# Hybrid decoder trunk on one core: other priorities for the parts of both mixers, and small DVE operations priced as users of the port shared with POOL

## The chip, the cores and the metric

The kernel runs on one core of one Trainium2 chip. The metric is the device time of one execution in microseconds (us); lower is better. A core has five engines that run at the same time, each through its own queue in order: TensorE (PE: matrix products and transposes), VectorE (DVE), ScalarE (ACT), GpSimd (POOL) and SyncE (SP, which here issues all DMA transfers). An engine waits for another through semaphores. Products land in banks of PSUM, and DVE or ACT move them to SBUF ("evict" them) before a bank can be used again. POOL and DVE share a port to SBUF.

## The reference

Two layers over a sequence of 512 rows of 1024 numbers, in float32. Each layer has a mixer, an MLP and a gated embedding, with layer norms between.

```python
for i in range(DEPTH):                       # DEPTH = 2
    m = _even_mixer(...) if i % 2 == 0 else _odd_mixer(...)
    x = _layer_norm(DN_ALPHA * x + m, ln1_g[i], ln1_b[i])
    x = _layer_norm(DN_ALPHA * x + _sq_relu_mlp(x, w_up[i], w_down[i]), ln2_g[i], ln2_b[i])
    gate = jax.nn.sigmoid(x @ ple_w_gate[i] + ple_b_gate[i])
    x = x + gate * (p[i] @ ple_w_proj[i])
```

The even mixer projects x once and feeds two kinds of attention. Eight latent heads (MLA) take queries from a query latent of 384 columns and keys and values from a kv latent of 256 columns; both latents are divided by their root mean square first. A rotary part of 32 columns is added to queries and keys. Eight sliding-window heads (SWA, window 128) share two key and value heads, with a table of relative position biases on the logits and a learned sink to each softmax. The odd mixer has sixteen causal heads whose logits get a cumulated forget gate. Each mixer ends in an output projection.

## The kernel before

**Numbers.** Every float32 value that enters a product is split into a rounded part ("hi", by a cast on ACT) and the rest ("lo", a subtraction on DVE or POOL); a product is three matmuls (hi·hi, hi·lo, lo·hi) into one bank (`mm3`). Weights come as pieces of up to 128 x 1024 through `piece`: a DMA into `raw`, a cast to `wh` (line 551), a subtraction to `wl` (line 488, on POOL or DVE as `SPLIT` and `on_pool` say). The function `weights` runs five pieces ahead; the operations that load and split a piece are recorded in the part that asked for weights at that moment. There are two `raw` buffers and twelve `w` buffers (six pieces).

**Stages.** The start loads x and three pieces and makes the shared keys and two of four sliding-window query pairs. Then come the even mixer's parts, its output projection with the first layer norm, the MLP with the second, the gated embedding, and the same with the odd mixer for the second layer.

**Parts.** `EVEN` and `ODD` list the parts of the two mixers. In the even one: `q` (projection of one pair of window queries; `q_stack`, lines 751 to 755, evicts it in two halves with two ACT casts and one DVE subtraction each), `kv` and `qn` (the latents' inputs, one block of 128 rows each; line 1016 copies the block), `ckv` and `cq` (division by the root mean square and transposes: line 1022, `rsqrt` with lines 631 to 640, POOL's scaling on line 1026, the products' eviction on lines 1036 and 1037), `rk` (rotation and transposes of the rotary key; lines 1058 and 1060 evict them as `kh` and `kl`), `bias` (the table of biases and the sinks), `c` (three DMA loads: the rotary tables and the causal mask), `v` (values), `r` (rotary queries, line 926), `mk` and `mq` (keys and queries of a pair of latent heads; `mq` also copies rotary rows by eight DMAs), `s` and `m` (one sliding-window or latent head: logits, softmax, transposes, product with the values), `os` and `om` (splits of the heads' outputs). In the odd one: `Q`, `K`, `V` (projections), `G` (forget gates), `F` (one head), `O` (split of outputs).

**What sets the order.** The program first records all operations with their engine, an estimated duration, and what they read and write (`Plan.op`). An operation's priority is its place in the record plus the shift of its part, and the smallest goes first:

```python
o.seq = len(self.ops)
o.prio = o.seq + self.shift
```

`Plan.schedule` then plays the program through on estimated durations. At each step it takes the engine that can go on first and, of that engine's operations that are ready at that time (inputs made, buffers free), the one with the smallest priority. Operations marked `port` share one more resource, and the delay is added after the choice:

```python
if o.port:
    t = max(t, port_free)
    port_free = t + o.dur
```

The order found in this way is fixed on each engine by dependences; on the chip an engine runs its operations in that order, whatever the actual durations are. In the kernel before, all operations on POOL are marked `port`, and on DVE those large ones that take all their inputs from SBUF (`tt`, and `split` with `psum=False`, and lines 1226, 1237, 1417, 1418). The weight pieces lie in memory in the order of the lists' names, not by priority.

**Layer norm** (`layer_norm`, lines 1220 to 1237): per block of 128 rows, sums of squares on ACT (line 1223), then a few operations on a single column: `nm` (1220), `va` (1228), a square root on ACT (1231), a reciprocal (1232), and one Newton step (1233 to 1235). Two large operations per half finish it (1226 and 1237), and PE transposes the result (line 523).

Of the kernel before, what the change touches and what calls it, by code (L numbers as in the profile page):

```python
# [34 lines left out]
ALU = mybir.AluOpType  # L35
# [12 lines left out]
        (5, 10, ((0, 1, 2), (3, 4, 5), (6, 7))),  # L48
        (10, 16, ((0, 1), (2, 3), (4, 5), (6, 7))))

EVEN = ("q1 bias+484 kv0-292 kv1-60 qn0+452 kv2-296 kv3+64 rk-132 qn1-692 qn2+272 qn3-104 s0+164 s1+292 ckv-156 "
        "c-204 q3-240 s2-124 s3-36 v0-56 s4+204 s5+224 cq-392 v1-84 s6+8 v2-84 v3-96 os0-204 r-72 s7+56 mk0+784 "
        "mq0-520 m0-284 m1+104 mk1+132 mq1-104 os3+804 os2-220 m2+132 m3-28 mk2-108 mq2-448 om0-192 m4-156 "
        "os1+1028 m5-260 mk3-276 om2+36 mq3-188 m6-104 m7-212 om3+144 om1-580").split()
ODD = ("Q0+88 V0-104 V1-240 V2+400 V3+1404 V4+1280 V5+2072 V6+1060 V7-1396 G+4 V8-196 V9-156 V10+704 K0-812 "
       "K3-1684 F0-304 Q4+1704 Q1-880 K1-420 F2+236 V11-1204 F1-1376 Q2-468 K2+360 F4-456 F5+120 K4+1484 F3-644 "
       "Q3+68 F6-1352 F7-384 F8-1156 K7+280 F9-372 Q5+332 K5-184 F10-1236 Q6-1004 F11-172 K6+68 F12-268 Q7+68 "
       "F13+44 O4-2576 O3+1208 F14-564 O0-532 F15-68 O5-704 O6-492 O2+840 O1-404 O7+2500").split()
EVEN_Q = 2
START = "x0 002 x1 104 x2 024 204 048 x3 x5 x4 x6 148 x7 248".split()  # L60
WARM = 8
# [4 lines left out]
def parts(order):  # L66

    for x in order:
        name, i, shift = re.fullmatch(r"([A-Za-z]+)(\d*)([+-]\d+)?", x).groups()
        yield name, [int(i)] if i else [], int(shift or 0)  # L70
# [23 lines left out]
def weight_pieces():  # L94
# [58 lines left out]
    own = {"q": e_q, "kv": e_kv, "qn": e_qn, "v": e_v, "r": e_r, "mk": e_mk}  # L153
    for name, i, _ in parts(EVEN):
        if name in own:
# [16 lines left out]
    def o_q(j, b=0):  # L172
        add(D, lambda I: _cols(I["od_w_in"][0], slice(b + j * P, b + (j + 1) * P)))

    own = {"V": o_v, "Q": o_q, "K": lambda j: o_q(j, D)}
    for name, i, _ in parts(ODD):
        if name in own:
# [250 lines left out]
def t_pe(n):  # L428
    return max((n + 32) / 2.4, 109.5) * 1e-3


class Trunk:
# [194 lines left out]
    def rsqrt(self, y, v, r, w, n=1, scale=0):  # L627

        t, hv = self.small("nt", n), self.small("nh", n)
        d = lambda fn, rr, ww, dur=0.07: self.dve(1, fn, rr, ww, dur=dur)  # L630
        d(lambda e: e.tensor_scalar(y().bitcast(I32), v().bitcast(I32), 1, None, ALU.arith_shift_right), r, [w])
        d(lambda e: e.tensor_scalar(hv[:], v(), -0.5 / 4 ** scale, None, ALU.mult), r, [hv])
        d(lambda e: e.tensor_scalar(y().bitcast(I32), y().bitcast(I32), -1, 0x5F3759DF + (scale << 23), ALU.mult, ALU.add), [], [w])
        for _ in range(3):
            if n == 1:
                d(lambda e: e.tensor_scalar(t[:], y(), y(), hv[:], ALU.mult, ALU.mult), [w, hv], [t], 0.19)
            else:
                d(lambda e: e.tensor_tensor(t[:], y(), y(), ALU.mult), [w], [t])
                d(lambda e: e.tensor_tensor(t[:], t[:], hv[:], ALU.mult), [hv], [t])
            d(lambda e: e.scalar_tensor_tensor(y(), t[:], 1.5, y(), ALU.add, ALU.mult), [t], [w])  # L640
# [137 lines left out]
    def even(self):  # L778
        self.start()
        for name, i, self.p.shift in parts(EVEN):  # L780
            getattr(self, "e_" + name)(*i)
# [55 lines left out]
    def e_bias(self):  # L837

        A, nc = self.A, self.nc
        oh = self.load("u", (P, 384), lambda: A["onehot"], "oh")  # L840
        rb = self.load("u", (P, P), lambda: A["relb"], "rb")
        pe = self.bank("o")
        self.pe(4 * t_pe(384), lambda: [nc.tensor.matmul(pe[:, :384], rb[:], oh[:], start=True, stop=True)], [rb, oh], [pe])
        et = self.u("e", F, (P, 384))
        self.dve(384, lambda e: e.tensor_copy(et[:], pe[:, :384]), [pe], [et])
        for i in range(2):
            self.dma(196608, lambda i=i: (self.scratch["e"].rearrange("(h i r w) -> i h r w", h=8, i=2, r=16)[i], et[:]),
                     [et], [(self.dram["e"], i)])
        self.sinks = self.load("sm16", (P, 8), lambda: A["sinks"].broadcast_to([P, 8]), "sinks")
        self.nsinks = self.p.buf("sm16", (P, 8), F, "nsinks")  # L850
        self.dve(8, lambda e: e.tensor_scalar(self.nsinks[:], self.sinks[:], -1.0, None, ALU.mult), [self.sinks], [self.nsinks])

    def e_q(self, j):
        b = self.bank("mm")
# [274 lines left out]
    def odd(self):  # L1129
# [5 lines left out]
        self.fq, self.fk, self.fo = {}, {}, {}  # L1135
        for name, i, self.p.shift in parts(ODD):
            getattr(self, "o_" + name.lower())(*i)
# [77 lines left out]
    def layer_norm(self, x, st, g, b):  # L1215

        nm, q, v, y = (self.small(n, 4) for n in ("nm", "sq", "va", "rs"))
        c = lambda z: z[:, 0:1]
        d = lambda fn, r, w, dur=0.07: self.dve(1, fn, r, w, dur=dur)
        d(lambda e: e.tensor_scalar(c(nm), st[:, 0:1], st[:, 1:2], -1.0 / D, ALU.add, ALU.mult), [st], [nm], 0.1)  # L1220
        for h in range(2):
            junk = self.u("junk")
            self.act(S, lambda e, h=h, junk=junk: e.activation(junk[:], x[h][:], AF.Square, bias=c(nm), accum_out=q[:, h:h + 1]),
                     [x[h], nm], [junk, (q, h)], aps=2)
        for h in range(2):
            self.dve(S + 57, lambda e, h=h: e.scalar_tensor_tensor(x[h][:], x[h][:], c(nm), g[h][:], ALU.add, ALU.mult),
                     [nm, g[h]], [x[h]], port=True)
        d(lambda e: e.scalar_tensor_tensor(c(v), q[:, 0:1], D * EPS, q[:, 1:2], ALU.add, ALU.add), [q], [v], 0.1)

        hv, t = self.small("hv", 4), self.small("nt", 4)  # L1230
        self.act(1, lambda e: e.activation(c(t), c(v), AF.Sqrt, scale=1.0 / D), [v], [t])
        d(lambda e: e.reciprocal(c(y), c(t)), [t], [y], 0.1)
        d(lambda e: e.tensor_scalar(c(hv), c(v), -0.5 / D, None, ALU.mult), [v], [hv])
        d(lambda e: e.tensor_scalar(c(t), c(y), c(y), c(hv), ALU.mult, ALU.mult), [y, hv], [t], 0.19)
        d(lambda e: e.scalar_tensor_tensor(c(y), c(t), 1.5, c(y), ALU.add, ALU.mult), [t], [y], 0.1)
        for h in range(2):
            self.dve(S + 57, lambda e, h=h: e.scalar_tensor_tensor(x[h][:], x[h][:], c(y), b[h][:], ALU.mult, ALU.add),
                     [y, b[h]], [x[h]], port=True)
# [255 lines left out]
```

## Time and profile before

| what | value |
|---|---|
| median of 3 runs | 1263.97 us (1263.49 to 1265.16) |
| the profiled execution's own time | 1265.41 us |
| its span, first to last instruction | 1263.6 us |
| PE busy | 1233.4 us (98%) |
| DVE busy | 949.7 us (75%) |
| ACT busy | 687.2 us (54%) |
| POOL busy | 505.2 us (40%) |
| mean granted clock of TensorE | 0.995 |

A busy share is an average over stages with different limits. A row of instructions gives its start and length in us, the engine, the line of the kernel, the operation, its tiles (out<-in), its shapes and, in brackets, how long the engine stood idle before it and what ended that. A row of waits gives the engine and line that waited, what it waited for, the total in us, the number of times and the longest. The line is often that of a helper: line 512 is every matmul of `mms`, 523 every transpose, 488 every `tt`, 502 and 503 the two halves of `split`.

### The profile page before, as it was taken

The page shows a single profiled execution, that of the slowest core. Times are in us where ns is not written, and L with a number is a line of the kernel's source. Part 1 is how long each engine was busy: PE and PEld are TensorE (multiplying, and loading weights), DVE is VectorE, ACT ScalarE, POOL GpSimd, SP SyncE. Part 2 cuts the span into 40 slices and gives each one's busy share as a digit, 9 for nine tenths or more (in the row PEclk, how much of TensorE's full clock was granted, in tenths as well). Part 3 has the DMA queues.
Part 4 walks back from the last instruction along what each step waited for, and adds up shares of the span by engine and source line. Part 5 has one row for each costly group of instructions (what it writes and reads, how often), then busy time and mean ns, then how long its engine had stood idle before and what let it go on. Part 6 is the DMA issues. An engine that isn't in the chain of part 4 may idle for free.

```text
span 1263.6 us, 17349 instructions
## 1 busy us (share of the span) xinstructions
PE 1233.4 (98%) x6108; PEld 1042.6 (83%) x6108; DVE 949.7 (75%) x1695; ACT 687.2 (54%) x1352; POOL 505.2 (40%) x408
## 2 busy tenths in 40 slices
PE   8988999999999999999999999899999999999998
PEld 6987888988888887888897888788888888888887
DVE  5568877899888887585543587868899878897564
ACT  5658874645444445353444697945654554445451
POOL 2545432444445444312213466331544545443120
PEclk9999999999999999999999999999999999999999
DMA  5422432233223422423232422352223332332131
GB/s 197 141 88 85 145 122 85 83 101 123 89 89 100 133 75 76 154 65 131 91 104 93 147 70 92 134 183 68 84 84 114 120 100 84 117 117 82 68 117 50
DMA packets 46791, 132.83 MB, mean 105 GB/s; under 512 B 5984, under 2 KB 8672, under 8 KB 46704
## 3 DMA queue, kind: packets, MB, share of 16 engines
q1 hardware_dynamic: 46704, 131.72, 31.6%
q8 instruction: 48, 0.79, 0.3%
q14 instruction: 39, 0.32, 0.1%
HBM read 126.03 MB, written 4.62 MB: 103 GB/s over the span
## 4 chain that ended last, share of the span: by engine, by line
PE 81%; ACT 8%; DVE 6%; issue 2%; DMA 2%; POOL 1%; SPq 0%; ACTq 0%; DVEq 0%; POOLq 0%
PE mm L512 31%; PE s L512 21%; PE t L512 16%; PE o L512 10%; ACT t L664 2%; PE t L523 2%; ACT wh L551 1%; DVE wl L488 1%; DMA raw<-in_wall_dram 1%; ACT pth L502 1%; DVE qlo L753 1%; ACT q L755 1%; ACT q L752 1%; DVE t L659 1%; POOL wl L488 0%
## 5 line engine op out<-in xcount | busy, mean ns | idle before, releaser
L488 POOL TENSOR_TENSOR wl<-raw,wh 128x1024 fp32r<-128x1024 f32 (+4 forms) x78 | 182.4, 2340 | 405.5 <-ACT wh L551 376.4
L551 ACT CAST wh<-raw 128x1024 fp32r<-128x1024 f32 (+5 forms) x150 | 152.2, 1018 | 148.0 <-DMA raw<-in_wall_dram 73.7
L488 POOL TENSOR_TENSOR wf<-raw,wf 128x512 fp32r<-128x512 f32 x84 | 122.1, 1475 | 173.4 <-ACT wf L584 156.8
L512 PE MATMUL mm<-xh,wh 128*128 128x512 f32 (+1 forms) x416 | 161.7, 389 | 2.8 <-DVE k L766 0.8
L512 PE MATMUL mm<-xl,wh 128*128 128x512 f32 (+1 forms) x416 | 159.6, 384 | 0.2 <-DVE xl L503 0.2
L512 PE MATMUL mm<-xh,wl 128*128 128x512 f32 (+1 forms) x416 | 159.7, 384 | 0.0
L488 DVE TENSOR_TENSOR wl<-raw,wh 128x1024 fp32r<-128x1024 f32 (+4 forms) x72 | 102.5, 1423 | 47.8 <-ACT wh L551 38.3
L584 ACT CAST wf<-raw 128x512 fp32r<-128x512 f32 x168 | 100.9, 615 | 34.9 <-PE t L512 15.3
L512 PE MATMUL t<-wf,rh 128*128 128x512 f32 x336 | 103.8, 390 | 0.7 <-DVE x L1350 0.7
L673 POOL TENSOR_SCALAR t<-t,st 128x256 f32<-128x256 f32 (+3 forms) x128 | 69.3, 561 | 79.3 <-DVE st L670 61.4
L512 PEld LDWEIGHTS mm<-xh,wh 128*128 128x128 f32 x416 | 78.8, 189 | 19.7 <-ACT q L755 2.2
L512 PEld LDWEIGHTS mm<-xh,wl 128*128 128x128 f32 x416 | 78.7, 189 | 15.8 <-DVE wl L503 0.4
L512 PEld LDWEIGHTS mm<-xl,wh 128*128 128x128 f32 x416 | 78.7, 189 | 14.4 <-DVE xl L503 0.5
L488 DVE TENSOR_TENSOR wf<-raw,wf 128x512 fp32r<-128x512 f32 x84 | 77.4, 936 | 17.4 <-ACT wf L584 17.1
L512 PE MATMUL mm<-wh,xh 128*128 128x384 f32 (+5 forms) x232 | 82.8, 357 | 5.9 <-DVE qlo L753 2.8
L512 PE MATMUL mm<-wl,xh 128*128 128x384 f32 (+5 forms) x232 | 80.6, 348 | 0.2 <-POOL wl L488 0.2
L512 PE MATMUL mm<-wh,xl 128*128 128x384 f32 (+5 forms) x232 | 80.7, 348 | 0.0
L1350 DVE TENSOR_TENSOR x<-x,t 128x512 f32<-128x512 f32 x100 | 67.0, 679 | 12.3 <-PE t L512 10.3
L664 ACT ACTIVATE t<-t,st 128x256 f32<-128x256 f32 (+3 forms) x128 | 68.7, 540 | 12.7 <-DVE st L659 10.6
L512 PEld LDWEIGHTS t<-wf,rh 128*128 128x128 f32 x336 | 62.8, 188 | 14.7 <-DVE x L1350 1.8
L512 PE MATMUL s<-wf,rh 128*128 128x512 f32 x224 | 69.0, 389 | 0.0
L512 PE MATMUL t<-wf,rl 128*128 128x512 f32 x168 | 65.4, 389 | 0.0
(296 smaller groups left out, 3273.9 us busy)
## 6 DMA issues: line engine op xcount, KB each, us to landing
raw<-in_wall_dram SPq DMA_DIRECT2D x183, 512.0 KB, 3.5
ck<-scratch_c SPq DMA_DIRECT2D x16, 256.0 KB, 3.8
raw<-in_wall_dram SPq DMA_DIRECT2D x9, 384.0 KB, 3.3
x<-in_xT_dram SPq DMA_DIRECT2D x8, 256.0 KB, 5.3
x<-in_xn_dram SPq DMA_DIRECT2D x8, 256.0 KB, 5.3
g<-in_rows_dram SPq DMA_DIRECT2D x8, 256.0 KB, 5.1
b<-in_rows_dram SPq DMA_DIRECT2D x8, 256.0 KB, 5.3
scratch_x<-x SPq DMA_DIRECT2D x8, 256.0 KB, 2.0
```

What stands on the lines that cost most here:

```text
L488: fn = lambda e: e.tensor_tensor(out(), a(), b(), op)
L502: self.act(n, lambda e: e.copy(hi(), src()), r, w, psum)
L512: return [self.nc.tensor.matmul(o(), a(), b(), start=s, stop=e, **kw) for o, a, b, s, e in prods]
L523: lambda: [self.nc.tensor.transpose(o(), i(), self.ident[:]) for o, i in items],
L551: self.act(w, lambda e: e.copy(hi[:, :w], raw[:, :w]), [raw], [hi])
L584: self.act(512, lambda e: e.copy(t[:, h[0]], src()), [key], [(t, 0)])
L659: return e.tensor_tensor_reduce(t[:, offs[i] + a:offs[i] + z], b[:, c + a:c + z], ad(), -scale, init, ALU.add, ALU.min, nm[:, i:i + 1])
L664: self.act(n, lambda e, i=i, tt=tt: e.activation(tt(), tt(), AF.Exp, bias=nm[:, i:i + 1], scale=-1.0, accum_out=sm[:, i:i + 1]), [(nm, i)] ...
L673: self.pool(0.13 + 1.21e-3 * n, lambda e, i=i, tt=tt: e.tensor_scalar(tt(), tt(), rc[:, i:i + 1], 1.0, ALU.mult, ALU.mult), [rc], [(t, i)])
L752: self.act(S, lambda e, q2=q2, rs=rs: e.copy(q2[rs, :], bank[rs, :]), [bank], [(q2, 0)], True)
L753: self.dve(S, lambda e, q2=q2, lo=lo, rs=rs: e.tensor_tensor(lo[rs, :], bank[rs, :], q2[rs, :].bitcast(F), ALU.subtract), [bank, (q2, 0)], ...
L1350: self.dve(S, lambda e, b=b, xx=xx: e.tensor_tensor(xx[:], xx[:], b[:], ALU.add), [b], [xx])
```

## The change

All parts stay in the same order of names, so the record and the weights' layout are the same; the shifts of 51 of 52 even parts and 24 of 53 odd parts change. In three places the small operations of DVE are recorded with `port=True`: in `rsqrt`, for `nsinks` in `e_bias`, and in `layer_norm`.

```diff
-EVEN = ("q1 bias+484 kv0-292 kv1-60 qn0+452 kv2-296 kv3+64 rk-132 qn1-692 qn2+272 qn3-104 s0+164 s1+292 ckv-156 "
-        "c-204 q3-240 s2-124 s3-36 v0-56 s4+204 s5+224 cq-392 v1-84 s6+8 v2-84 v3-96 os0-204 r-72 s7+56 mk0+784 "
-        "mq0-520 m0-284 m1+104 mk1+132 mq1-104 os3+804 os2-220 m2+132 m3-28 mk2-108 mq2-448 om0-192 m4-156 "
-        "os1+1028 m5-260 mk3-276 om2+36 mq3-188 m6-104 m7-212 om3+144 om1-580").split()
-ODD = ("Q0+88 V0-104 V1-240 V2+400 V3+1404 V4+1280 V5+2072 V6+1060 V7-1396 G+4 V8-196 V9-156 V10+704 K0-812 "
-       "K3-1684 F0-304 Q4+1704 Q1-880 K1-420 F2+236 V11-1204 F1-1376 Q2-468 K2+360 F4-456 F5+120 K4+1484 F3-644 "
-       "Q3+68 F6-1352 F7-384 F8-1156 K7+280 F9-372 Q5+332 K5-184 F10-1236 Q6-1004 F11-172 K6+68 F12-268 Q7+68 "
-       "F13+44 O4-2576 O3+1208 F14-564 O0-532 F15-68 O5-704 O6-492 O2+840 O1-404 O7+2500").split()
+EVEN = ("q1+12 bias+556 kv0-1128 kv1+20 qn0+440 kv2-244 kv3-156 rk-164 qn1-672 qn2-440 qn3-576 s0-116 s1+300 "
+        "ckv+132 c+536 q3-836 s2+108 s3+84 v0+16 s4+204 s5+956 cq-404 v1-160 s6+80 v2-32 v3-164 os0+532 r-68 "
+        "s7+152 mk0+2040 mq0-1268 m0+4 m1+236 mk1+184 mq1+16 os3+1272 os2-292 m2+224 m3-116 mk2+136 mq2-668 "
+        "om0-432 m4-608 os1+1368 m5-92 mk3-188 om2-4 mq3-1240 m6-72 m7-100 om3+216 om1-376").split()
+ODD = ("Q0+88 V0-104 V1-168 V2+400 V3+1404 V4+1280 V5+2072 V6+1020 V7-1396 G-76 V8-196 V9-156 V10+524 K0-812 "
+       "K3-1604 F0-304 Q4+1764 Q1-888 K1-420 F2+236 V11-1204 F1-1216 Q2-468 K2+352 F4-456 F5+120 K4+1404 F3-652 "
+       "Q3+68 F6-1352 F7-384 F8-1136 K7+248 F9-212 Q5+332 K5-144 F10-1236 Q6-1004 F11-552 K6+68 F12-276 Q7+68 "
+       "F13+44 O4-2436 O3+1428 F14-744 O0-840 F15+72 O5-656 O6-492 O2+840 O1-396 O7+2500").split()
@@ rsqrt
-        d = lambda fn, rr, ww, dur=0.07: self.dve(1, fn, rr, ww, dur=dur)
+        d = lambda fn, rr, ww, dur=0.07: self.dve(1, fn, rr, ww, dur=dur, port=True)
@@ e_bias
-        self.dve(8, lambda e: e.tensor_scalar(self.nsinks[:], self.sinks[:], -1.0, None, ALU.mult), [self.sinks], [self.nsinks])
+        self.dve(8, lambda e: e.tensor_scalar(self.nsinks[:], self.sinks[:], -1.0, None, ALU.mult), [self.sinks], [self.nsinks], port=True)
@@ layer_norm
-        d = lambda fn, r, w, dur=0.07: self.dve(1, fn, r, w, dur=dur)
+        d = lambda fn, r, w, dur=0.07: self.dve(1, fn, r, w, dur=dur, port=True)
```

## The prediction, made before the changed kernel ran

> **What bounds the kernel now.** I read the page first, then the busy time by stage, then what TensorE (PE) waited for in each stage. The first two rows are the page's, the others the busy time of each engine in five stretches (granted clock and DMA share at the end).
>
> ```profile
> span 1263.6 us, 17349 instructions
> PE 1233.4 (98%) x6108; PEld 1042.6 (83%) x6108; DVE 949.7 (75%) x1695; ACT 687.2 (54%) x1352; POOL 505.2 (40%) x408
> ```
> ```profile
> 0.00:30.00 30.00, 26.34 (x93) 18.16 (x94) 16.12 (x24) 16.53 (x26) 6.80 (x15) 0.94 0.60 197
> 30.00:190.00 160.00, 149.82 (x857) 132.93 (x857) 118.03 (x314) 117.23 (x293) 73.51 (x96) 0.98 0.36 117
> 190.00:630.00 440.00, 438.02 (x2083) 367.27 (x2082) 347.04 (x492) 213.37 (x374) 171.51 (x102) 1.00 0.31 100
> 630.00:840.00 210.00, 201.11 (x1095) 173.09 (x1094) 137.13 (x391) 140.83 (x309) 94.59 (x106) 1.00 0.36 118
> 840.00:1263.60 423.60, 418.12 (x1987) 351.13 (x1985) 331.38 (x476) 199.26 (x353) 158.83 (x91) 1.00 0.28 93
> ```
>
> PE sets the end: it is idle for 1263.6 - 1233.4 = 30.2 us in all. An order of work can only move idle time and slow stretches of PE, so the places are the even mixer behind its start (30 to 190 us, 10.2 us idle) and the odd mixer (630 to 840 us, 8.9 us). The start's 3.7 us belong to loads that neither list orders. Who ended PE's waits, in us, times and longest, first in 30 to 190, then in 630 to 840:
>
> ```profile
> PE mm L512 <- DVE ql L503: 4.3, 4, 3.2
> PE mm L512 <- DVE kl L1060: 2.1, 1, 2.1
> PE mm L523 <- DVE qlo L753: 1.2, 1, 1.2
> PE mm L512 <- DVE qlo L753: 0.9, 1, 0.9
> ```
> ```profile
> PE t L523 <- DVE ptl L503: 3.0, 3, 1.1
> PE mm L512 <- DVE qlo L753: 1.6, 2, 0.8
> PE s L512 <- DVE st L659: 1.2, 1, 1.2
> PE s L512 <- ACT q L755: 1.0, 1, 1.0
> ```
>
> Two waits are long, and both are for a "mm" bank that VectorE (DVE) had not emptied: 2.06 us before 66.19 and 3.17 us before 118.37. Behind each comes a second cost. These are PE's rows at the two places, and the windows after them (the third number from the end is the granted clock):
>
> ```profile
> 66.19 0.41 PE L512 MATMUL mm<-wh,xh 128*128 128x384 f32 x1 [2.06 <-DVE kl L1060]
> 118.37 0.76 PE L512 MATMUL mm<-ch,wh 128*128 128x512 f32 x1 [3.17 <-DVE ql L503]
> ```
> ```profile
> 67.00:70.40 3.40, 3.40 (x12) 3.40 (x11) 3.40 (x9) 2.26 (x11) 3.40 (x6) 0.50 0.00 0
> 118.20:121.60 3.40, 3.23 (x9) 2.68 (x10) 3.25 (x10) 2.53 (x10) 2.04 (x5) 0.50 0.47 112
> ```
>
> For 3.4 us after each of these waits the clock is 0.50, which costs 3.4 x 0.5 = 1.7 us more. The shorter waits have no such stretch: the clock of 0.98 over the 160 us is 3.2 us lost, these two and no third. So the first place costs 2.06 + 1.7 = 3.8 us and the second 3.17 + 1.7 = 4.9 us, together 8.7 of the 13.6 us (10.2 idle, 3.4 of slow clock) that any order of the even mixer could win. The Trainium skill (TensorE: Matmul & The Clock Gate, section "Why this matters for your kernels") asks for no idle gaps over about 3 us between bursts of matmuls; here 2.06 us was enough, so the trace differs and its row is used. By the page alone the first place would be worth 2.06 us, and the time 1261.9.
>
> **The change part by part.** No instruction comes or goes; only the order on each engine does, as the planner now prices and ranks it.
>
> *The port.* 121 operations now count as users of the port shared with GpSimd (POOL): 12 in each of the two `rsqrt` calls, `nsinks`, and 6 in each of 16 layer norms. Do they block? Rows of the lines concerned, with durations in ns as least/median/greatest:
>
> ```profile
> L638 DVE TENSOR_TENSOR nt<-rn x6: 156/162/2400, 59.3 to 89.9; 128x4 f32<-128x4 f32 x6
> ```
> ```profile
> L1228 DVE SCALAR_TENSOR_TENSOR va<-sq x16: 145/151/2384, 203.9 to 1209.1; 128x1 f32<-128x1 f32 x16
> ```
> ```profile
> L851 DVE TENSOR_SCALAR nsinks<-sinks x1: 1955/1955/1955, 18.7 to 18.7; 128x8 f32<-128x8 f32 x1
> ```
>
> They do: an operation of 0.16 us lasts up to 2.40 us. The longest `nt` sits just ahead of the first long wait. DVE's order there, and POOL's operation of that time:
>
> ```profile
> 61.17 2.40 DVE L638 TENSOR_TENSOR nt<-rn 128x4 f32<-128x4 f32 x1
> ...
> 64.08 0.68 DVE L503 TENSOR_TENSOR ptl<-t,pth 128x512 fp32r<-128x512 f32 x1
> 64.68 1.37 DVE L1060 TENSOR_TENSOR kl<-mm,kh 32x512 fp32r<-32x512 f32 x2
> ```
> ```profile
> 61.15 2.40 POOL L488 TENSOR_TENSOR wl<-raw,wh 128x1024 fp32r<-128x1024 f32 x1 [4.14 <-ACT wh L551]
> ```
> ```profile
> 61.64 1.16 ACT L1058 CAST kh<-mm 32x512 fp32r<-32x512 f32 x2
> 62.82 0.58 ACT L716 COPY ol<-o 64x512 f32<-64x512 f32 x1
> 63.42 0.48 ACT L502 CAST pth<-t 128x384 fp32r<-128x384 f32 x1
> ```
>
> POOL's split of q3's weight piece holds `nt` from 61.17 to 63.57, inside the reciprocal root of the kv latent. `kl`, which frees the bank, has had its input since 62.8 but stands behind `ptl`, and `ptl` waits for `pth` until 63.90. Bounds: with the block gone and the order kept, `ptl` could start at about 63.95 instead of 64.08, a gain of 0.13 us; with `kl` ahead of `ptl` and no block, `kl` could run from 62.8 to 64.2, PE would start 1.9 us sooner, the wait would be 0.2 us, and the slow stretch would not come: 3.8 us. The lower side is also open: more such blocks could fall elsewhere (a rival). I take 3.8 us, because what stood around the place is moved apart. A part's rank is the number of operations before it plus its shift. By count, `ckv` (this root) goes from 168 to 456, behind `s0` and `cq`; `kv0`, which carries q3's weight split, from -156 to -992; `qn2` from 510 to -202 and `qn3` from 144 to -328; `rk`, which holds `kl`, stays early (90 to 58).
>
> *Layer norms.* Four of 16 `va` are blocked (2.36 to 2.38 us). PE feels two of them:
>
> ```profile
> 230.00 0.55 PE L523 MATMUL t<-ident,x 128*128 128x128 f32 x3 [0.92 <-DVE x L1237]
> ```
> ```profile
> 878.69 0.55 PE L523 MATMUL t<-ident,x 128*128 128x128 f32 x3 [0.88 <-DVE x L1237]
> ```
>
> Bounds: -1.8 us if both go, +1.8 us if each doubles. I take 0: the planner picks by rank and readiness first and only then adds the port's delay, so `va` still follows `x` in line, and those ranks do not change.
>
> *q3.* It goes from 116 to -480, ahead of `cq` (112). Its 24 matmuls of 0.227 us cost the same anywhere; its bank does not. Its first and last evictions, and PE's wait for the bank:
>
> ```profile
> 90.42 0.58 ACT L752 CAST q<-mm 64x512 fp32r<-64x512 f32 x1 [1.42 <-PE mm L512]
> ...
> 93.55 0.69 DVE L753 TENSOR_TENSOR qlo<-mm,q 64x512 fp32r<-64x512 f32 x1 [1.24 <-ACT q L755]
> 94.39 0.52 PE L523 MATMUL mm<-ident,cn 128*128 128x128 f32 x3 [1.20 <-DVE qlo L753]
> ```
>
> The bank is held from 90.42 to 94.24, 3.82 us, of which other work (value products, `ckv`'s products, sink heads) hides all but 1.20. Bounds: -1.20 if the new neighbours hide it all, 3.82 - 1.20 = +2.6 if nothing does, and +1.7 for the slow clock on top. I take 0: a move with cover on both sides.
>
> *mq0, mq3, m4, c, s5.* `mq0` (151 to -597) and `mq3` (757 to -295) cannot run before the query latent and, for their rotary rows, part `r`; each issues 8 copies of about 0.6 us on the DMA queue (SP). `c` (149 to 889) issues three loads there, with about 60 us to spare now, so a later issue costs nothing until it is later than its 3.9 us of landing before `r`; then `r` and all eight heads wait. The first copy, and the rows of these loads and their first user:
>
> ```profile
> 111.72 0.62 SPq L495 DMA_DIRECT2D qh<-rh  x1
> ```
> ```profile
> L926 DVE TENSOR_TENSOR rt<-mm,rope x4: 680/686/692, 106.9 to 109.6; 128x512 f32<-128x512 f32 x4
> L495 SPq DMA_DIRECT2D rope<-in_rope_dram x2: 422/425/428, 43.2 to 43.6; - x2
> ...
> DMA to landing us min/median/max: 3.9/3.9/4.0
> ```
>
> Weight loads queue behind these copies on SP, but the pieces are fetched five ahead. `m4` passes `m0` (712 to 260, against 402 to 690) and `s5` sinks (709 to 1441). These re-deal the second long wait (4.9 us) without a row that says how. Bounds -4.9 and +4.9 (a second of its kind); I take 0.
>
> *Odd mixer.* 29 of 53 shifts stay and 15 move by 80 or less (a head has 37 operations); the largest moves are `F11` (-380), `O0` (-308) and `O3` (+220). The longest waits there are 1.2 us, none slows the clock. Bounds: half of the 8.9 us idle either way would be 4.4; I take 0 and let about 1.2 us (one wait) into the spread.
>
> **Sum.** -3.8 (first place) + 0 + 0 + 0 + 0. The profiled execution took 1265.41 us, of which 1263.6 is span and 1.8 lies around it; it becomes 1261.6. The median of the runs shown is 1263.97, 1.44 below it; the forecast is 1263.97 - 3.8 = 1260.2.
>
> **Rivals.**
> *Deeper (D):* the second long wait goes too. For it: it is a `ql` behind work of other parts on ScalarE (ACT), and `mq0` and `mq3` now outrank these. Against: `r`, which they need, stays where it was. 1260.2 - 4.9 = 1255.3.
> *Re-dealt (N):* waits of the same total elsewhere; the change does not do what it says, since planned order decides and the block meets another small operation. For it: the two `rsqrt` calls make 24 small operations, and POOL is busy 73.5 of 160 us there. 1264.0.
> *Slower (S):* q3 is evicted with nothing to hide it. One mechanism: both "mm" banks are full while `qn` or `kv` blocks want one, the 3.82 us hold is bare, and the clock halves behind it. It decides once PE's other work in the hold is under 1.8 us (a wait over 2 us). Price with the first place kept: 3.82 - 1.20 + 1.7 = +4.3, so 1268.3. For it: at -480 q3 stands among `qn` and `kv`, all users of the two banks, and sink heads, which hid it, are few that early. Against: its weight piece is loaded behind `qn`'s.
> *Over-priced (R):* some of the 121 never block. At 563.75 a reciprocal of the layer norm ran through in POOL's operation:
>
> ```profile
> 563.75 0.15 DVE L1232 RECIPROCAL rs<-nt 128x1 f32<-128x1 f32 x1
> ```
> ```profile
> 562.10 2.42 POOL L488 TENSOR_TENSOR wl<-raw,wh 128x1024 fp32r<-128x1024 f32 x1 [5.42 <-ACT wh L551]
> ```
>
> The planner now delays such operations by up to 2.4 us that the chip does not, so work that could go first stands behind them; doubling PE's two waits on `x` gives +1.8, so 1265.8. The Trainium skill (SBUF — State Buffer, section "Who interferes with whom") says that a DVE instruction with at most one SBUF input, outside its two-port modes, does not contend with GpSimd; by that rule this is R's case, and the reciprocal agrees at 0.15 us.
>
> **Chances.** Forecast 0.36, D 0.19, N 0.17, R 0.05, S 0.23. A measurement of this kernel tells about 0.2%, 2.5 us. Faster is the forecast and D, 0.55; within 0.2% is N and R, 0.22; slower is S, 0.23. The forecast's own range is 1258.5 to 1261.4. The range of 8 in 10 goes from D with 1.5 us below it (the odd mixer's one wait and a little) to S with 0.5 above: 1253.8 to 1268.8. It leaves out the far ends: both long waits and all layer-norm waits gone, or `c` landing late.
>
> **What would show it.** Right: no wait for `kl` over 1 us and no window at clock 0.50 between 60 and 75 us; PE idle in the even mixer down by about 2 us; PE busy time down by the slow stretch (1.7). Layer norms: `va` still at 2.38 four times, waits on `x` near 0.9. S: a `qlo` wait over 2 us before 100 us with a slow window behind it. D: one slow window fewer still. R: longer waits on `x`. The forecast is wrong if the slow windows after 30 us remain two, whatever became of `nt`.

## The result, and the profile after

The changed kernel takes 1256.81 us (median of 6 runs, 1256.37 to 1260.08) against 1263.84 us for the kernel before (median of 6 runs, 1262.53 to 1265.16). The ratio is 0.9947, with a 95% interval of 0.9935 to 0.996: faster by 5.1 to 8.2 us, most likely 6.7. The forecast was 1260.2 us in a range of 1253.8 to 1268.8. One execution of one later kernel (1525.14 us at a mean clock of 0.752, where the others of that kernel have 0.995 to 0.999) is left out of its time below.

The first two rows below are those of the page of the changed kernel, the others the busy time of each engine in the same five stretches as before, with TensorE's granted clock as the third number from the end.

```profile
span 1255.1 us, 17347 instructions
...
PE 1231.3 (98%) x6108; PEld 1040.5 (83%) x6108; DVE 943.9 (75%) x1695; ACT 686.9 (55%) x1352; POOL 505.5 (40%) x408
```
```profile
0.00:30.00 30.00, 27.54 (x105) 19.35 (x106) 17.37 (x25) 18.34 (x29) 6.79 (x15) 1.00 0.62 209
30.00:190.00 160.00, 152.07 (x872) 134.31 (x871) 123.25 (x320) 116.57 (x292) 73.81 (x96) 0.99 0.38 120
190.00:630.00 440.00, 438.11 (x2096) 368.34 (x2095) 341.22 (x490) 214.50 (x378) 171.56 (x101) 1.00 0.30 99
630.00:840.00 210.00, 203.93 (x1095) 174.78 (x1095) 135.63 (x395) 139.49 (x304) 96.73 (x106) 1.00 0.36 120
840.00:1255.10 415.10, 409.63 (x1948) 343.75 (x1946) 326.41 (x467) 197.97 (x351) 156.57 (x90) 1.00 0.29 93
```

PE is idle for 1255.1 - 1231.3 = 23.8 us, 6.4 less than before. In the even mixer (30 to 190 us) the idle time is 7.9 in place of 10.2 us, in the odd mixer (630 to 840 us) 6.1 in place of 8.9; the two long stages between and behind them barely differ. What PE waited for in the two mixers of the changed kernel (total, times, longest, in us):

```profile
PE mm L512 <- DVE ql L503: 3.9, 3, 2.7
PE mm L523 <- DVE qlo L753: 1.2, 1, 1.2
PE mm L523 <- DVE vsw L503: 1.1, 1, 1.1
...
PE mm L512 <- DVE kl L503: 0.2, 1, 0.2
```
```profile
PE t L523 <- DVE ptl L503: 1.8, 2, 0.9
PE s L512 <- DVE st L659: 1.5, 2, 1.2
```

The wait for `kl` of line 1060 is gone altogether (the `kl` that is left comes from line 503, another part). In the odd mixer one of the three waits for `ptl` is gone, and so is that of 1.0 us for `q`.

Stretches of fixed bounds hold a little more or less work in the two kernels, so I also read the lengths between landmarks: the first start of line 752 (the first query pair is evicted), the first start of line 1152 (the odd mixer's forget gates) and the last start of line 1220 (the last block of the last layer norm). Each row gives its first and last start, here of before and then of after.

```profile
L752 ACT CAST q<-mm x22: 565/581/585, 25.4 to 809.5; 64x512 fp32r<-64x512 f32 x22
L1152 DVE COPY fn<-mm x4: 174/175/176, 618.5 to 640.6; 128x16 f32<-128x16 f32 x4
L1220 DVE TENSOR_SCALAR nm<-st x16: 197/214/216, 201.4 to 1206.2; 128x1 f32<-128x1 f32 x16
```
```profile
L752 ACT CAST q<-mm x22: 564/580/583, 22.9 to 802.2; 64x512 fp32r<-64x512 f32 x22
L1152 DVE COPY fn<-mm x4: 174/174/175, 611.9 to 633.8; 128x16 f32<-128x16 f32 x4
L1220 DVE TENSOR_SCALAR nm<-st x16: 198/214/215, 194.9 to 1197.4; 128x1 f32<-128x1 f32 x16
```

From the first `q` to the first `fn`, the even mixer and what follows it in the first layer, is 593.1 us before and 589.0 after: -4.1. From there to the last `nm`, the odd mixer and what follows, is 587.7 and 585.5: -2.2. The first `q` itself comes 2.5 us earlier (25.4 and 22.9), but neither list orders the work ahead of it, and the kernels below, whose work ahead of it is the same, have it anywhere from 22.6 to 25.0, three that keep the lists of before at 22.6 to 23.1: this pair of profiles shows a difference of 2.5 us there that isn't the change's. Most of it is slow clock: in the profile of before the granted clock is 0.90 from 5 to 10 us and 0.76 from 10 to 15 (5 x 0.10 + 5 x 0.24 = 1.7 us lost), in that of after it is 1.00 in both, and the only other kernel with such a start is the one at 25.0. Without these 2.5 us the profiles differ by 6.0 us, near the 6.7 of the ratio.

One more landmark tells where in the first layer the gain lies, the first start of line 926 (the rotary queries, between the two long waits). It is 106.9 before; after it is:

```profile
L926 DVE TENSOR_TENSOR rt<-mm,rope x4: 680/685/690, 100.5 to 103.4; 128x512 f32<-128x512 f32 x4
```

From the first `q` to there the length falls from 81.5 to 77.6 us, and PE's idle time in it from 6.4 to 4.4 us at a clock of 0.98 and then 1.00 (422 and 417 matmuls fall into it, so some 1 us is work that moved behind it). From there to the first `nm`, the stretch with the second long wait, it is 94.5 and 94.4, with 500 and 503 matmuls and 4.9 and 4.7 us idle at 0.98 in both. The idle time and the half clock that the first layer lost lie at the first place.

How the first place looks now, on DVE and on POOL:

```profile
58.05 0.17 DVE L638 TENSOR_TENSOR nt<-rn 128x4 f32<-128x4 f32 x1
...
59.03 1.38 DVE L1060 TENSOR_TENSOR kl<-mm,kh 32x512 fp32r<-32x512 f32 x2 [0.62 <-ACT kh L1058]
60.44 1.99 DVE L640 SCALAR_TENSOR_TENSOR rn<-nt,rn 128x4 f32<-128x4 f32 x1
```
```profile
60.03 2.38 POOL L488 TENSOR_TENSOR wl<-raw,wh 128x1024 fp32r<-128x1024 f32 x1 [2.24 <-ACT wh L551]
```

The block has not gone: POOL's split of a weight piece still holds a small operation of the reciprocal root, now `rn` for 1.99 us. But it falls behind `kl`, which waits for nothing but its own input. The second place is still there, its wait a little shorter. These are PE's row and, right behind it, the window at half clock:

```profile
112.18 0.47 PE L512 MATMUL mm<-ch,wh 128*128 128x512 f32 x1 [2.69 <-DVE ql L503]
```
```profile
112.90:116.30 3.40, 3.40 (x13) 3.03 (x13) 2.63 (x6) 1.72 (x7) 2.17 (x5) 0.50 0.35 89
```

### The profile page after: what moved, and what is told of

Same layout as the page of the kernel before. It is cut to its first block, busy times and chain, and to the rows that moved or that the text cites. A ratio compares the mean times of both kernels' runs of the same rounds, so it can differ in the third digit from the quotient of the medians.

```text
span 1255.1 us, 17347 instructions
## 1 busy us (share of the span) xinstructions
PE 1231.3 (98%) x6108; PEld 1040.5 (83%) x6108; DVE 943.9 (75%) x1695; ACT 686.9 (55%) x1352; POOL 505.5 (40%) x408
## 4 chain that ended last, share of the span: by engine, by line
PE 84%; ACT 7%; DVE 5%; issue 2%; DMA 1%; POOL 1%; SPq 0%; ACTq 0%; DVEq 0%; POOLq 0%
PE mm L512 32%; PE s L512 22%; PE t L512 17%; PE o L512 10%; ACT t L664 2%; PE t L523 2%; ACT pth L502 1%; ACT q L755 1%; DVE t L659 1%; DMA raw<-in_wall_dram 1%; ACT wh L551 1%; DVE qlo L753 1%; ACT q L752 1%; DVE ptl L503 1%; ACT ol L716 1%
```

## The experiments

Lengths of the two halves, read at the landmarks as above in each kernel's one profile, and the timed ratio to the kernel before:

| kernel | first `q` to first `fn` | first `fn` to last `nm` | ratio to before, 95% interval |
|---|---|---|---|
| before | 593.1 | 587.7 | 1 |
| changed | 589.0 | 585.5 | 0.9947 (0.9935 to 0.996) |
| price alone | 597.6 | 587.6 | 1.0042 (1.0026 to 1.0058) |
| shifts alone | 598.0 | 585.2 | 1.0035 (1.0023 to 1.0047) |
| price and new EVEN | 588.9 | 588.4 | 0.9962 (0.9947 to 0.9977) |
| price and new ODD | 599.0 | 585.3 | 1.0022 (1.0012 to 1.0033) |
| before, POOL's split moved | 589.7 | 588.6 | 0.9985 (0.9976 to 0.9994) |
| before, `kl` ahead (first try) | 593.0 | 588.7 | 0.9997 (0.9989 to 1.0006) |
| before, `kl` ahead (casts first) | 591.0 | 587.3 | 0.9989 (0.9979 to 0.9998) |
| changed, eviction of `mq0` first | 591.1 | 586.4 | 0.9963 (0.995 to 0.9976) |
| changed, room on DVE | 589.7 | 585.1 | 0.996 (0.9947 to 0.9973) |
| changed, layer norms not priced | 588.2 | 585.3 | 0.9943 (0.9931 to 0.9955) |

The second column shows how far one profile can be trusted: kernels with the old ODD list lie between 587.3 and 588.7, those with the new one between 585.1 and 586.4.

### Which half of the change carries it?

The price alone (the changed kernel with the two old lists):

```diff
-EVEN = ("q1+12 bias+556 kv0-1128 kv1+20 ...").split()
-ODD = ("Q0+88 V0-104 V1-168 V2+400 ...").split()
+EVEN = ("q1 bias+484 kv0-292 kv1-60 ...").split()
+ODD = ("Q0+88 V0-104 V1-240 V2+400 ...").split()
```

> The old shifts with the small operations priced as port users; nothing else of the change. Theory A (the price alone ends the first long wait, since the planner then puts kl ahead of the small operation that blocks): no PE wait for kl over 1 us between 55 and 75 us, even mixer about 3.8 us shorter there; the rest of the order is re-dealt with shifts that were not made for it, so 1257 to 1264. Rival B (the shifts end it): the wait for kl stays at about 2 us with a slow clock behind it, and the time is 1264 or more.

The shifts alone (the changed kernel without the three `port=True`):

```diff
-        d = lambda fn, rr, ww, dur=0.07: self.dve(1, fn, rr, ww, dur=dur, port=True)
+        d = lambda fn, rr, ww, dur=0.07: self.dve(1, fn, rr, ww, dur=dur)
```

and the same for `nsinks` and in `layer_norm`.

> The new shifts of both mixers without the price. Theory A: the planner does not know of the blocks, DVE's order around kl is made as if a small operation took 0.07 us, and most of the 7 us is lost again: 1261 to 1268. Rival B (the shifts carry the gain): 1256 to 1258.

The price with the new EVEN and the old ODD, and the price with the old EVEN and the new ODD:

> The price and the even mixer's new shifts, the odd mixer's old ones. By the two profiles the even mixer gave about 4.1 us of the gain and the odd one about 2.3 us: 1259 to 1260, and an odd mixer (first forget-gate copy to first layer norm behind it) of about 231 us as before the change. If the odd list's gain needs nothing of the price, the odd mixer is as long as in the kernel before; if the old odd list suffers under the price, it is longer.

> The price and the odd mixer's new shifts, the even mixer's old ones. Its even mixer is that of the price alone, its odd mixer that of the changed kernel (about 228.7 us from the first forget-gate copy to the first layer norm): so 2 to 3 us below the price alone, if the mixers do not act on each other.

Measured: each half alone makes the kernel slower, 1269.76 us for the price and 1267.48 for the shifts against 1263.53 before on the same chip. The even mixer wins only with both (1259.53 with the price and the new EVEN, 1266.49 with the price and the new ODD). Neither expectation of the halves held as it was argued: the price ended the long wait for `kl`, as theory A has it, but the time lies 6 us above theory A's range; the shifts alone lie in theory A's range, but not for its reason, since `kl` isn't late there. The odd mixer wins with its new list, priced (585.3) or not (585.2), so that part does not come from the price: of the waits near its end, which the kernel before has at 809.5, 816.5 and 823.0 us (0.99, 1.09 and 0.77), the changed kernel has one of 0.51 at 804.2.

What went wrong in the halves isn't the first place. With the price alone, first PE and then DVE:

```profile
63.41 0.41 PE L512 MATMUL mm<-wh,xh 128*128 128x384 f32 x1 [0.59 <-DVE kl L1060]
...
115.04 0.72 PE L512 MATMUL mm<-ch,wh 128*128 128x512 f32 x1 [3.60 <-DVE ql L503]
...
129.70 0.39 PE L512 MATMUL o<-pth,vsw 128*128 128x256 f32 x1 [1.99 <-DVE ots L717]
```
```profile
59.38 2.40 DVE L638 TENSOR_TENSOR nt<-rn 128x4 f32<-128x4 f32 x1
...
61.89 1.37 DVE L1060 TENSOR_TENSOR kl<-mm,kh 32x512 fp32r<-32x512 f32 x2
```

With the shifts alone, PE, then DVE, then a second window at half clock:

```profile
115.45 0.47 PE L512 MATMUL mm<-ch,wh 128*128 128x512 f32 x1 [4.05 <-DVE ql L503]
...
130.15 0.50 PE L512 MATMUL mm<-ch,wh 128*128 128x512 f32 x1 [2.00 <-DVE kl L503]
```
```profile
58.90 1.37 DVE L1060 TENSOR_TENSOR kl<-mm,kh 32x512 fp32r<-32x512 f32 x2
```
```profile
150.20:153.60 3.40, 3.40 (x12) 2.90 (x11) 2.85 (x10) 2.39 (x8) 0.00 (x0) 0.51 0.96 304
```

Either half cuts the wait for `kl` in its own way. Under the price `nt` is blocked as before (2.40 us), but `kl` comes two operations behind it, no longer behind `ptl`: the wait is 0.59. Under the shifts the split falls behind `kl`. Both then lose more between 100 and 160 us than they won: waits of 3.60 and 1.99, or 4.05, 2.00 and (at 148.8) 1.96, where the changed kernel has 2.69 and nothing else over 1 us. PE's idle time by stretches of the first layer shows the same (clock in brackets; each stretch holds a few matmuls more or less from kernel to kernel):

| kernel | first `q` to first `rt`, idle us | first `rt` to first `nm`, idle us | its length, us |
|---|---|---|---|
| before | 6.4 (0.98) | 4.9 (0.98) | 94.5 |
| changed | 4.4 (1.00) | 4.7 (0.98) | 94.4 |
| price alone | 4.8 (1.00) | 9.4 (0.98) | 100.4 |
| shifts alone | 5.1 (1.00) | 9.7 (0.97) | 99.4 |

So the long wait for `kl` is gone in every kernel that has the price or the new EVEN, and what decides the sign is how the evictions fall behind the first `rt`. Why just this pair deals them well isn't settled by these runs.

### Is the block the cause of the wait for kl?

Kernel before with every engine's order kept, but POOL's subtraction for q3's weight piece behind the two POOL operations that followed it. A few lines behind the planner move operations in its finished order; this and the next kernels differ in what they move.

```diff
+def moved(self, first=Plan.schedule):
+    order = first(self)
+    for seq, behind in MOVES:
+        o = next(x for x in order if x.seq == seq)
+        order.remove(o)
+        order.insert(next(i for i, x in enumerate(order) if x.seq == behind) + 1, o)
+    return order
+
+
+MOVES = ((147, 395),)
+Plan.schedule = moved
```

> The kernel before with every engine's order kept, but for POOL's subtraction of q3's weight piece, which now follows the two POOL operations that stood behind it. Nothing then holds the port when nt (L638) of the kv latent runs. Block theory (the blocked nt delays ptl, and with it kl): nt lasts 0.16 instead of 2.40 us, kl starts near 62.5 to 62.8 instead of 64.68, PE's wait of 2.06 us for kl falls under 0.4, the clock of 0.50 at 67 us does not come; 2.0 to 3.8 us faster, 1259.9 to 1261.7. The prediction's reading (ptl waits for a pth that ends at 63.90 anyway, so that the block alone is worth 0.13 us): kl still starts at about 64.5, the wait stays near 1.9, no change within 0.5 us. Rival: the split is late for its own users and PE waits for wl in place of kl: slower by 1 to 3 us.

Measured: 1261.6 us against 1263.22, ratio 0.9985, 0.8 to 3.0 us faster. DVE and PE at the place:

```profile
58.85 0.16 DVE L638 TENSOR_TENSOR nt<-rn 128x4 f32<-128x4 f32 x1
...
59.52 0.68 DVE L503 TENSOR_TENSOR ptl<-t,pth 128x512 fp32r<-128x512 f32 x1
60.50 1.38 DVE L1060 TENSOR_TENSOR kl<-mm,kh 32x512 fp32r<-32x512 f32 x2 [0.30 <-ACT kh L1058]
```
```profile
62.02 0.41 PE L512 MATMUL mm<-wh,xh 128*128 128x384 f32 x1 [0.19 <-DVE kl L1060]
```

The block theory holds, and the prediction's reading of the order does not. `nt` lasts 0.16 us, `ptl` follows without waiting, `kl` waits only for its own cast, and PE's wait falls from 2.06 to 0.19 us with no stretch at half clock behind it. `ptl` had not waited for the cast `pth` that ended at 63.90 in the kernel before; it needs the one of 61.17, and the cast of 63.42 feeds a later `ptl`. The shapes say it as well: this `ptl` is 128x512, the cast of 63.42 is 128x384. So the block alone was worth the wait, not 0.13 us. The timed gain, 1.9 us, is as large as the 2.06 - 0.19 of idle time, and its interval leaves at most 3.0 - 1.9 = 1.1 us for the 1.7 us of half clock. The mean granted clock points the same way: 0.9978 over the 12 runs of this kernel and 0.9972 over the runs of before beside it (without one whose clock was recorded as 0.946), a difference worth about 0.0006 x 1261 = 0.7 us, though this mean also holds slow stretches elsewhere, such as that of the start. An explanation that fits, and that no run here tests by itself, is that the stretch does not stand behind the wait in every execution.

The same place by order alone: in the kernel before, `kl` goes ahead of `ptl`, the block stays.

```diff
+MOVES = ((225, 334), (227, 225))
```

> The kernel before with every engine's order kept, but on DVE the eviction kl (L1060, first of rk) goes ahead of the subtraction ptl that stood between nt and it; the block on nt stays. Order theory (the shared port matters only by what stands behind the blocked operation): kl starts near 64.0 instead of 64.68, PE's wait falls from 2.06 to about 1.4 us, and PE then waits for the later ptl by up to 0.7. If the slow clock needs about 2 us of idle, the window at 67 us goes: 1.7 to 2.4 us faster, 1261.2 to 1261.9. If a wait of 1.4 us is enough for it, or the ptl behind it costs what kl gains: within 0.7 us of before.

Measured: 1262.79 us, no difference. The theory isn't tested by it, since the edit brought a wait of its own. ACT's second cast and PE's wait:

```profile
62.74 0.57 ACT L1058 CAST kh<-mm 32x512 fp32r<-32x512 f32 x1 [3.27 <-DVE kl L1060]
```
```profile
63.36 0.44 PE L512 MATMUL mm<-wh,xh 128*128 128x384 f32 x1 [1.96 <-ACT kh L1058]
```

In the finished order of this kernel both `kl` stood ahead of the second cast `kh`, which reads the same bank, and the cast waited 3.27 us for them. With the casts put ahead again:

```diff
+MOVES = ((226, 334), (225, 226), (227, 225))
```

> The kernel before with DVE's kl (L1060) again ahead of the subtraction ptl, and in the record both casts kh ahead of both kl, as in the kernel before, so that the second cast no longer stands behind kl. The block on nt stays. Order theory: kl starts near 64.0 on the kernel before's scale (0.68 us earlier than before), PE's wait falls from 2.06 to about 1.4 us. If the clock of 0.50 needs about 2 us of idle, the window there goes as well: with the 0.7 us of wait 0.7 to 2.4 us faster. If 1.4 us is enough: 0.7 us faster, not to be told from no change.

Measured: 1262.33 us against 1263.57, ratio 0.9989, 0.3 to 2.7 us faster.

```profile
58.54 2.39 DVE L638 TENSOR_TENSOR nt<-rn 128x4 f32<-128x4 f32 x1
...
61.45 1.38 DVE L1060 TENSOR_TENSOR kl<-mm,kh 32x512 fp32r<-32x512 f32 x2
```
```profile
62.97 0.41 PE L512 MATMUL mm<-wh,xh 128*128 128x384 f32 x1 [1.46 <-DVE kl L1060]
```

The block of 2.39 us is still there, and PE's wait falls by the 0.6 us that `kl` is earlier, to 1.46. That wait has no half clock behind it in this profile. So both count: the block, whose removal took 1.9 us out of the wait of 2.06, and what stands behind it, worth 0.6 of the wait.

### Can the second place be repaired?

DVE and then ACT of the changed kernel ahead of the wait of 2.69 us at 112.18:

```profile
107.14 1.22 DVE L488 TENSOR_TENSOR wl<-raw,wh 128x1024 fp32r<-128x1024 f32 x1
108.39 0.69 DVE L503 TENSOR_TENSOR ql<-mm,qh 64x512 fp32r<-64x512 f32 x1
...
111.35 0.68 DVE L503 TENSOR_TENSOR ql<-mm,qh 64x512 fp32r<-64x512 f32 x1
```
```profile
107.04 0.58 ACT L502 CAST qh<-mm 64x512 fp32r<-64x512 f32 x1
...
110.73 0.58 ACT L502 CAST qh<-mm 64x512 fp32r<-64x512 f32 x1
```

The bank is emptied in two halves, and 2.96 us lie between the two `ql`. First try: the second half goes ahead of other parts' work.

```diff
+MOVES = ((678, 573), (679, 624))
```

> The changed kernel with every engine's order kept, but the second half of mq0's eviction (the cast qh on ACT and the subtraction ql on DVE) goes ahead of the softmax and value work of other parts that stood in front of it. If PE's wait of 2.69 us at 112.2 us is that eviction's place in line alone: the wait falls to 0.4 to 1.2 us, the clock of 0.50 at 113 us does not come, 1.5 to 4 us faster than the changed kernel: 1253 to 1255.3. If the waits only move to the transposes and logits whose evictions are now later: within 1 us of the changed kernel, 1256 to 1258, with new waits for t, st or ptl of together over 2 us between 110 and 130 us.

Measured: 1258.84 us against 1263.22 for before, ratio 0.9963; the interval overlaps that of the changed kernel, and its first half of the program (591.1) is 2.1 us longer. PE's waits there:

```profile
112.14 0.47 PE L512 MATMUL mm<-ch,wh 128*128 128x512 f32 x1 [1.83 <-DVE st L669]
...
114.86 0.39 PE L512 MATMUL o<-ptl,vsw 128*128 128x256 f32 x1 [0.98 <-DVE ptl L503]
...
117.05 0.50 PE L512 MATMUL s<-kl,qh 96*128 96x512 f32 x1 [0.88 <-DVE kl L503]
```

No half clock follows in this profile, but 1.83 + 0.98 + 0.88 = 3.7 us stand in place of 2.69. Second try: DVE's split of 1.22 us leaves the line ahead of the first `ql` and goes behind the next `kl`; the load that waits for its buffer goes behind the next copies on SP; the second half follows the first; two `ptl` go ahead of two of the T additions.

```diff
+MOVES = ((506, 636), (509, 506), (664, 645), (842, 765), (678, 685), (679, 484))
```

> The changed kernel with every engine's order kept but for six moves between 107 and 117 us: the 1.22 us subtraction of a weight piece of the output projection leaves DVE's line ahead of mq0's evictions and goes behind the next kl; the load that waits for its buffer goes behind the next copies on SP; the second half of mq0's eviction follows the first with ol alone between; two ptl go ahead of two of the T additions. If the wait of 2.69 us is DVE's full line there: it falls under 1.2 us, no clock of 0.50 at 113 us, the waits for ptl and kl behind it stay together under 1.5 us; 2 to 4 us faster than the changed kernel, 1253 to 1255. If ACT's line or the copies set the same end: the waits move to kl, ptl or the logits' qh, 1256 to 1259.

Measured: 1258.26 us against 1263.57, ratio 0.996, no better than the changed kernel.

```profile
110.78 0.47 PE L512 MATMUL mm<-ch,wh 128*128 128x512 f32 x1 [1.12 <-DVE st L670]
...
115.52 0.50 PE L512 MATMUL s<-kl,qh 96*128 96x512 f32 x1 [1.95 <-DVE kl L503]
```

PE goes on 1.4 us earlier at the first wait, as expected, and loses it again: `kl` waits for its cast on ACT, which has the softmax in front of it (in this kernel ACT is busy for 8.50 and DVE for 7.90 of the 10 us from 107; in the changed one it is 7.95 and 8.68). In these two tries, whichever bank is emptied first, another comes late: DVE and ACT are both 79 to 87% busy there. That no order of the two lines would do better isn't shown. Neither try beats the changed kernel.

### Does the layer norms' price matter?

```diff
@@ layer_norm
-        d = lambda fn, r, w, dur=0.07: self.dve(1, fn, r, w, dur=dur, port=True)
+        d = lambda fn, r, w, dur=0.07: self.dve(1, fn, r, w, dur=dur)
```

> The changed kernel with the price left on the small operations of the two reciprocal roots and of nsinks alone; the layer norms' operations are not counted as users of the port. Worked through in the planner, the orders of the even and of the odd mixer are then those of the changed kernel, and only the stages behind the mixers differ. If the price helps only where a block stands on TensorE's path: the stage from the last of the even mixer to the first fn and from the odd mixer to the end is within 1 us of the changed kernel, 1256 to 1258. If the layer norms' price carries part of the gain (the waits for x at 230 and 879 us that went): 1258 to 1260, and two waits of about 0.9 us for x L1237 are back. If the planner holds work behind operations that the chip does not block (the over-priced rival): faster than the changed kernel by 1 to 2 us, 1254.5 to 1256.

Measured: 1256.2 us against 1263.57, ratio 0.9943 (0.9931 to 0.9955), not to be told from the changed kernel's 0.9947. One of the two waits for `x` is back:

```profile
869.42 0.66 PE L523 MATMUL t<-ident,x 128*128 128x128 f32 x4 [0.89 <-DVE x L1237]
```

The changed kernel has waits of 0.52 and 0.34 there instead, for `xh` and `xl`, which add up to the same 0.9. So 96 of the 121 priced operations do nothing that shows in the time; the price works through the two reciprocal roots (and `nsinks`, which was not tried apart from them).

## Why the prediction was right or wrong

**The bound and the places: right.** PE is idle 6.4 us less, and 5.1 us of that is in the two mixers (2.3 and 2.8). Another 1.2 us is in the first 30 us (3.7 before, 2.5 after), which the change does not order. PE's busy time is down by 2.1 us, but not by the one stretch that was named for it (1.7): the start's slow clock is 1.7 of the difference too, and from the first `q` to the last `nm` the busy time falls by only 1.1 (1157.7 to 1156.6).

**The first place: the sum right, its reading wrong.** The forecast took 3.8 us as the upper end of two bounds. The even part came out at -4.1 us in the profiles, nearly all of it ahead of the first `rt`, and with the price and the new EVEN alone the timed ratio of 0.9962 is -4.8 us (2.9 to 6.7). The signs named for it are there: no wait for `kl` over 1 us, no window at 0.50 between 60 and 75 us, idle time in the even mixer down 2.3 us. The step that failed is "`kl` stands behind `ptl`, and `ptl` waits for `pth` until 63.90", and with it the lower bound of 0.13 us. Removing the block is worth 1.9 us (0.8 to 3.0) by time. I had matched the `ptl` to the cast of the same name that ended nearest ahead of it; in a line of equal names the order of the record tells which belongs to which. The half clock behind the wait is gone from the profile, as forecast, but over many executions it was worth at most 1.1 us in the kernel with the split moved, not 1.7. That the sum of 3.8 us came out is in part luck: the reason given for taking the upper end, that the ranks move apart what stood around the place, holds for the shifts without the price as well, and there the wait also goes and the kernel is 4.4 us slower.

**What the price does: not told.** The prediction put the gain down to the ranks and gave the price of the reciprocal roots no effect of its own. The ranks did move the block behind `kl`, and the shifts alone do that as well; the price alone repairs the place too, through the order of `kl` and `ptl`. In the even mixer neither wins without the other, and the prediction, which costed the change place by place, had no term for that. Its rival N (waits re-dealt elsewhere, 1264.0) comes nearest to what each half does by itself, but the new waits are larger than the old: 1267.48 and 1269.76 us.

**Layer norms at 0: near in the sum, wrong in the count.** Two `va` are blocked, not four (2.40 us at 863.7 and 2.36 at 1193.1), while the waits for `x` of 0.92 and 0.88 became waits of 0.34 for `xl` and of 0.52 and 0.34 for `xh` and `xl`, 1.2 us in place of 1.8. The first of the two went without the layer norms' price as well, so it is not the price's. The price did reorder the others, which the prediction held it could not: without it a third `va` is blocked (2.36 us at 547.5), and the second wait for `x` is back.

**q3 at 0, and the rival S: the 0 right, its reason not.** With a rank of -480 q3 hardly moved against its neighbours (its first eviction comes 62.0 us behind the first `q`, 65.1 before), and its bank costs what it did (1.20 before):

```profile
88.87 0.52 PE L523 MATMUL mm<-ident,cn 128*128 128x128 f32 x3 [1.23 <-DVE qlo L753]
```

The 0 was taken for a move with cover on both sides, and the move did not come. The argument against S, that q3's weight piece is loaded behind `qn`'s, does not explain it by itself: the piece is split by 62.41 us (POOL's row of the changed kernel, 60.03 and 2.38 long) and q3's first product comes at 79.14. The planner gives a bank to a part only when more banks of that name are free than parts recorded ahead of it still want, which could be what holds q3; no run here tests it.

**`mq0` and its neighbours at 0, and the rival D: nearly right.** The second long wait went from 3.17 to 2.69 us, and its stretch at half clock stayed. The stretch around it is no shorter (94.5 and 94.4 us). In the two attempts above `mq0`'s evictions went ahead of other parts' and made those late, so D needs more than that.

**The odd mixer at 0: the term that was mis-sized.** It is -2.2 us by the landmarks, with bounds of 4.4 either way, and it is the main reason why 1256.8 lies below the forecast's own range of 1258.5 to 1261.4: with the old ODD the price and the new EVEN take 1259.53, inside it. The new ODD list took out 0.99 + 1.09 + 0.77 - 0.51 = 2.3 us of waits at the end of the mixer; which of its shifts did it was not tried. The prediction gave it one wait's spread of 1.2 us; three waits in a row at one end of a stage, 2.85 of its 8.9 idle us, were the row to look for.

**Over-priced (R): not seen.** Without the layer norms' price the time is the same. By the Trainium skill (SBUF — State Buffer, section "Who interferes with whom") a DVE instruction with two inputs from SBUF contends with a GpSimd instruction that reads SBUF, and one with at most one such input does not, outside the two-port modes. The rows agree: `nt` and `rn`, with two inputs, were held for 2.40 and 1.99 us, the reciprocal of before ran through in 0.15. `nsinks`, with one tensor input, was held as well (1.96 us beside a split on POOL from 18.52 to 20.58); the exception of the two-port modes leaves room for that, and no run here shows in which mode it ran. To price all 12 operations of a root alike may be more than the chip asks, but it cost nothing that these runs can tell.

## What to carry to other kernels

Read a blocked instruction by what stands behind it: move the blocker, or move the one eviction that PE waits for ahead of it, and price the wait by its idle time first (here 1.9 us), with only a part of the half clock on top. When a planner's costs and its priorities change together, test each alone before saying what won: here each half alone lost 0.35 to 0.42%, and the pair gained 0.53%. Where two evicting engines are both some 80% busy, an eviction moved forward can make another late, and the waits then only change their names, as in both tries here. And match an operation with its source by order and shape, not by the name that ended last.

## What the runs showed of the hardware

A wait does not decide by its length alone whether TensorE's clock halves behind it. The kernel whose layer norms aren't priced has the order of the changed kernel in the even mixer, and the same wait. PE's row, and the window behind it:

```profile
112.62 0.47 PE L512 MATMUL mm<-ch,wh 128*128 128x512 f32 x1 [2.69 <-DVE ql L503]
```
```profile
112.40:115.80 3.40, 2.92 (x16) 2.37 (x17) 2.79 (x10) 3.07 (x10) 3.12 (x5) 1.00 0.34 89
```

The clock stays at 1.00, where the changed kernel's profile has 0.50 for 3.4 us behind a wait of 2.69. On the other side the first try of `kl` ahead was slowed behind a wait of 1.96 us:

```profile
64.00:67.40 3.40, 3.40 (x12) 3.40 (x12) 3.25 (x9) 3.40 (x12) 3.40 (x5) 0.50 0.02 2
```

Waits of 1.95 (room on DVE) and 1.99 us (price alone) were not followed by one; of two waits of 2.00 us one was (price and new ODD, at 131.1) and one was not (shifts alone, at 130.15). The seven waits of 3.16 to 4.05 us behind the start in these profiles all were. So between 1.96 and 2.69 us these profiles show both, for the same order too, which fits that removing a wait of 2.06 us won its idle time and at most part of the half clock. By the Trainium skill (TensorE: Matmul & The Clock Gate, section "Why this matters for your kernels") gaps over about 3 us between bursts of matmuls are to be avoided; the rows agree above 3 us and add that shorter ones are slowed some of the time.
